# Sixteen of 22 row tiles of a down projection as seven products of quarters, in three of four SwiGLU half-steps

## The chip, the cores and the metric

The kernel runs on one core of a Trainium2 chip. The metric is the time of one execution on the device in microseconds (us). An engine's name is short here: PE is the tensor engine, PEld its weight load, DVE the vector engine, ACT the scalar engine, POOL the GpSimd engine, SP the engine whose queue issues the transfers.

## The reference: what is computed

A two-layer encoder trunk on 512 tokens of width 1024. Each layer has a SwiGLU half-step, a token mixer and another SwiGLU half-step, each followed by a layer norm. The change concerns the second, third and fourth of the four half-steps (the first one keeps its code). Cut to that, the reference is

```
def swiglu(x, w_gate, w_up, w_down):            # [512,1024], [1024,2816] twice, [2816,1024]
    return (jax.nn.silu(x @ w_gate) * (x @ w_up)) @ w_down

x = layer_norm(DEEPNORM_ALPHA * x + 0.5 * swiglu(x, w_gate[l, i], w_up[l, i], w_down[l, i]),
               ln_g[l, 2 * i], ln_b[l, 2 * i])
```

## The kernel before, in words

Tokens lie in NT = 4 tiles of 128 and the hidden width 2816 in NF = 22 row tiles of 128. Every float32 product is three products of float32r numbers: each operand is split into hi (a rounded copy, made by ACT in `split`, line 90) and lo = x - hi (made by DVE, line 92), and `mm3` (lines 122 to 124) sums hi*hi, hi*lo and lo*hi in PSUM. A product of one 128x128 stationary tile with 512 columns is thus three matmul instructions.

`ffn` is one half-step. Its up part runs over fg = 0 to 10, two row tiles of the hidden width at a time: four weight loads of 512 KB (two of the gate weights, two of the up weights), each split into a pair of tiles `whi`, `wlo`, then 96 matmuls of 512 columns into four PSUM banks. ACT's tanh (line 251) and three DVE operations (lines 252 and 254, and the lo of the split) turn the four banks into the activations `act` of two row tiles, hi and lo. At fg = 0 some token tiles of x are still to be transposed; there the columns are worked in two halves of 256 tokens, with the transposes (`flush`, line 131) between them.

Its down part runs over the 22 row tiles of `w_down`: one load of 512 KB, one split, and 4 token tiles x 2 column halves x 3 = 24 matmuls into all eight PSUM banks. The last four row tiles are held back and done token tile by token tile, so that the layer norm of one token tile (`ln_tile`) runs under the next one's matmuls. `ln_tile` begins with two DVE operations (line 158) that add 0.25 times a bank to `xt`, the tile that holds alpha*x; `self.pending` then keeps the transposes of the normed tile for the next stage.

The weights come through pools that turn round: four `raw` buffers (`fetch`, line 104), five `whi` and five `wlo` (`halves`), eight PSUM banks. A load is issued by SP when DVE has finished with the `raw` buffer it gets, and ACT splits into a `whi` when the matmuls that read it are done. Every engine takes its instructions in a fixed order that a scheduler has written down at build time; only in a block under `as_written` is PE's order the order of the program. In the half-steps 2 to 4 of the kernel before nothing is under `as_written`.

Of the kernel before, what the change touches and what calls it, by code (L numbers as in the profile page):

```python
# [2 lines left out]

# [12 lines left out]
P = 128  # L16
# [31 lines left out]
class Trunk:  # L48
    """Every float32 product runs as three float32r passes: each operand is split exactly into
    hi (rounded to float32r) and lo = x - hi, and hi*hi + hi*lo + lo*hi is summed in PSUM."""  # L50
# [21 lines left out]
    @contextmanager  # L72
    def as_written(self, *engines):
        """The engines take what the block traces in the order of the program."""
# [38 lines left out]
    def load_next(self):  # L113
        """the next phase's first weights, ahead of it"""
        if self.coming:
            self.got, got = [], self.got
            got.append(self.load(*self.coming.pop(0)))
            self.got = got

    def mm3(self, ps, ah, al, bh, bl, start, stop):  # L120
        mm = self.nc.tensor.matmul
# [14 lines left out]
    def rstd(self, var, scale, eps):  # L136
        """(scale*var + eps) ** -0.5 on [128, 1]"""
# [13 lines left out]
    def ln_tile(self, t, z, p0, p1, yscale, g, b, out=None, spill=None):  # L151
        """z holds alpha*x of token tile t; x <- LayerNorm(z + yscale*y), then alpha*x into z.
        The transposes wait in self.pending, so that the tensor engine has other work first."""
        nc = self.nc
        s = self.sm.tile([P, 6], F32, name="st")
        for h, p in enumerate((p0, p1)):
            zz = z[:, h * 512:(h + 1) * 512]
            nc.vector.scalar_tensor_tensor(out=zz, in0=p, scalar=yscale, in1=zz, op0=ALU.mult, op1=ALU.add,
                                           accum_out=s[:, h:h + 1])
# [3 lines left out]
        for h, p in enumerate((p0, p1)):  # L163
# [23 lines left out]
    def flush(self, keep=0):  # L187
        """the waiting transposes, but for the last few"""
# [3 lines left out]
    def cols(self, bks, stat, a=0, b=SEQ):  # L192
        """Products of weight columns with x^T, for tokens a..b."""
# [5 lines left out]
    def load_x(self, x, xt):  # L199
        """x and the first weights; the transposes of the later tokens wait in self.pending"""  # L200
# [79 lines left out]

    def out_proj(self, W, stat, order, get_z, g_ap, b_ap, spill=None):
        """x <- LayerNorm(alpha*x + y @ W), y given transposed as [hi, lo] tiles of 128 rows.
        Runs up to the next yield with each step; stat[c] must be there when chunk c has its turn."""
# [38 lines left out]
    def gelu2(self, y, out, tmp):  # L322
        """out = 2*gelu(y) (tanh form); y may be in PSUM, out and tmp in SBUF."""
# [880 lines left out]
```

## Time and profile before

| | |
|---|---|
| median of 3 runs | 1848.93 us (1847.23 to 1849.03) |
| span of the profiled execution, first to last instruction | 1845.7 us |
| what lies around the span, median less span | 3.2 us |
| PE busy, PEld busy | 1818.3 us, 1523.2 us |
| DVE busy, ACT busy | 898.4 us, 637.0 us |
| matmul instructions | 8896 |
| mean granted clock of PE | 0.998 of full speed |

Busy time counts an instruction from its start to its end, and instructions of one engine that follow closely overlap a little: a distance from start to start is what an engine needs per instruction in a dense stretch. A share of the span is a mean over stages with different limits, so the stage itself has to be looked at.

### The profile page before, as it was taken

The page shows a single profiled execution, that of the slowest core. Times are in us where ns is not written, and L with a number is a line of the kernel's source. Part 1 is how long each engine was busy: PE and PEld are TensorE (multiplying, and loading weights), DVE is VectorE, ACT ScalarE, POOL GpSimd, SP SyncE. Part 2 cuts the span into 40 slices and gives each one's busy share as a digit, 9 for nine tenths or more (in the row PEclk, how much of TensorE's full clock was granted, in tenths as well). Part 3 has the DMA queues.
Part 4 walks back from the last instruction along what each step waited for, and adds up shares of the span by engine and source line. Part 5 has one row for each costly group of instructions (what it writes and reads, how often), then busy time and mean ns, then how long its engine had stood idle before and what let it go on. Part 6 is the DMA issues. An engine that isn't in the chain of part 4 may idle for free.

```text
span 1845.7 us, 22332 instructions
## 1 busy us (share of the span) xinstructions
PE 1818.3 (99%) x8896; PEld 1523.2 (83%) x8896; DVE 898.4 (49%) x1531; ACT 637.0 (35%) x971; POOL 32.2 (2%) x119
## 2 busy tenths in 40 slices
PE   8999999999999999999999999999999999999998
PEld 7888888888877888888889888888878898888886
DVE  7856542267766644433227334432388554343324
ACT  3233421246675432222115223221264332222211
POOL 0000000000000000000000000000010000000000
PEclk9999999999999999999999999999999999999999
DMA  6345623264412633332323333323333153333231
GB/s 206 105 125 166 205 96 103 91 193 132 153 55 92 205 115 100 95 102 93 98 97 104 102 94 100 97 98 93 118 101 104 47 149 92 103 92 103 92 103 57
DMA packets 158968, 206.48 MB, mean 112 GB/s; under 512 B 7696, under 2 KB 129808, under 8 KB 158864
## 3 DMA queue, kind: packets, MB, share of 16 engines
q1 hardware_dynamic: 158864, 205.06, 36.3%
q8 instruction: 69, 1.13, 0.3%
q14 instruction: 35, 0.29, 0.0%
HBM read 189.83 MB, written 14.16 MB: 111 GB/s over the span
## 4 chain that ended last, share of the span: by engine, by line
PE 72%; issue 22%; DVE 3%; ACT 1%; DMA 1%; POOL 1%; POOLq 0%; SPq 0%; DVEq 0%; ACTq 0%
PE ps L122 23%; PE ps L123 23%; PE ps L124 23%; PE ps L131 1%; PE ps L650 1%; DVE wlo L92 1%; DMA s5tl<-side 1%; PE ps L698 0%; POOL rs L141 0%; PE ps L690 0%; DMA x<-in_x_dram 0%; DVE pl L92 0%; ACT ps L164 0%; PE ps L689 0%; ACT whi L90 0%
## 5 line engine op out<-in xcount | busy, mean ns | idle before, releaser
L92 DVE TENSOR_TENSOR wlo<-raw,whi 128x1024 fp32r<-128x1024 f32 x313 | 382.6, 1222 | 593.0 <-ACT whi L90 592.0
L122 PE MATMUL ps<-xh,whi 128*128 128x512 f32 (+1 forms) x1696 | 635.9, 376 | 0.7 <-ACT xh L90 0.7
L123 PE MATMUL ps<-xl,whi 128*128 128x512 f32 (+1 forms) x1696 | 633.4, 374 | 2.8 <-DVE xl L92 2.8
L124 PE MATMUL ps<-xh,wlo 128*128 128x512 f32 (+1 forms) x1696 | 633.2, 374 | 0.0
L90 ACT ACTIVATE whi<-raw 128x1024 fp32r<-128x1024 f32 x313 | 330.7, 1058 | 823.0 <-PE ps L123 470.3
L122 PEld LDWEIGHTS ps<-xh,whi 128*128 128x128 f32 x1696 | 319.2, 189 | 59.8 <-issue 3.1
L123 PEld LDWEIGHTS ps<-xl,whi 128*128 128x128 f32 x1696 | 320.3, 189 | 58.0 <-DVE xl L92 3.3
L124 PEld LDWEIGHTS ps<-xh,wlo 128*128 128x128 f32 x1696 | 320.2, 189 | 56.7
L122 PE MATMUL ps<-whi,act 128*128 128x512 f32 x656 | 255.5, 390 | 0.0
L124 PE MATMUL ps<-whi,act 128*128 128x512 f32 x656 | 255.2, 389 | 0.0
L123 PE MATMUL ps<-wlo,act 128*128 128x512 f32 x656 | 255.2, 389 | 0.0
L124 PEld LDWEIGHTS ps<-whi,act 128*128 128x128 f32 x656 | 123.2, 188 | 25.5
L123 PEld LDWEIGHTS ps<-wlo,act 128*128 128x128 f32 x656 | 123.2, 188 | 25.4
L122 PEld LDWEIGHTS ps<-whi,act 128*128 128x128 f32 x656 | 123.2, 188 | 25.4
L252 DVE SCALAR_TENSOR_TENSOR th<-th,ps 128x512 f32<-128x512 f32 x88 | 59.8, 683 | 113.4 <-ACT th L251 113.4
L251 ACT ACTIVATE th<-ps 128x512 f32<-128x512 f32 x88 | 51.9, 595 | 155.1 <-PE ps L124 155.1
L254 DVE TENSOR_TENSOR th<-th,ps 128x512 f32<-128x512 f32 x88 | 59.7, 686 | 92.8 <-PE ps L124 92.8
L92 DVE TENSOR_TENSOR act<-th,act 128x512 fp32r<-128x512 f32 x82 | 52.7, 684 | 0.0
L122 PE MATMUL ps<-whi,xh 128*128 128x256 f32 (+1 forms) x160 | 49.6, 312 | 2.0 <-ACT whi L90 1.5
L123 PE MATMUL ps<-wlo,xh 128*128 128x256 f32 (+1 forms) x160 | 49.1, 307 | 2.2 <-DVE wlo L92 2.2
L90 ACT ACTIVATE act<-th 128x512 fp32r<-128x512 f32 x82 | 47.2, 617 | 7.6 <-DVE th L254 7.5
L124 PE MATMUL ps<-whi,xl 128*128 128x256 f32 (+1 forms) x160 | 48.5, 304 | 0.0
(303 smaller groups left out, 1360.2 us busy)
## 6 DMA issues: line engine op xcount, KB each, us to landing
raw<-in_wg_dram SPq DMA_DIRECT2D x88, 512.0 KB, 3.8
raw<-in_wu_dram SPq DMA_DIRECT2D x88, 512.0 KB, 3.8
raw<-in_wd_dram SPq DMA_DIRECT2D x88, 512.0 KB, 3.2
raw<-in_ab_in_dram SPq DMA_DIRECT2D x20, 512.0 KB, 4.5
raw<-in_cd_in_dram SPq DMA_DIRECT2D x12, 512.0 KB, 3.7
x<-in_x_dram SPq DMA_DIRECT2D x8, 512.0 KB, 6.7
s<-zf SPq DMA_DIRECT2D x8, 512.0 KB, 5.2
raw<-in_ab_out_dram SPq DMA_DIRECT2D x8, 512.0 KB, 4.2
```

The lines of the kernel that those rows point to most:

```text
L90: nc.scalar.activation(out=hi, in_=src, func=AF.Copy, scale=scale)
L92: nc.vector.tensor_tensor(out=lo, in0=src, in1=hi.bitcast(F32), op=ALU.subtract)
L122: mm(ps, ah, bh, start=start, stop=False)
L123: mm(ps, ah, bl, start=False, stop=False)
L124: mm(ps, al, bh, start=False, stop=stop)
L131: self.nc.tensor.transpose(p[:, j * P:(j + 1) * P], src[:, k * P:(k + 1) * P], self.ident)
L251: nc.scalar.activation(out=th, in_=bk[0, f], func=AF.Tanh, scale=0.5)
L252: nc.vector.scalar_tensor_tensor(out=th, in0=th, scalar=1.0, in1=bk[0, f], op0=ALU.add, op1=ALU.mult)
L254: nc.vector.tensor_tensor(out=th, in0=th, in1=bk[1, f], op=ALU.mult)
L650: nc.tensor.matmul(banks[h][:, o:o + w], a[r, i * P:i * P + P], b[r, :w], start=n == 0, stop=n == 2)
```

## The change

The half-steps 2 to 4 call `ffn7` instead of `ffn`. The first sixteen row tiles of the down part, in two groups of four pairs (pair j holds row tiles 2j and 2j+1), are no longer multiplied tile by tile. For a group, the activations are a 2x2 matrix of blocks (256 tokens by the even or the odd row tiles) and the weights a 2x2 matrix of blocks (even or odd row tiles by 512 columns), and the product of the two is made from seven products of blocks in place of eight (Winograd's form of Strassen's method). The factors are blocks or sums of blocks. The sums of activations are made by DVE at the end of each `up(fg)` (lines 345 to 348, into `hb`), so that a slot `sl` holds seven stationary factors, hi and lo, for a pair. The sums of weights are made by DVE from four loads (`w21`, `w11`, `w12`, `w22`, lines 384 to 387). A group has two units of two pairs. The seven products go, in the order of the code, into four pairs of banks Y, Z, X, V, and `take` adds a pair of banks to `xt` (line 162, the same operation as line 158 before); X is read out three times and V twice, and further products are summed onto what the banks hold. A group runs as soon as its fourth `up` is done: after fg = 3 and after fg = 7. Row tiles 16 to 21 are done as before. The whole of the up part and the two groups stand under `as_written`, so PE follows the program's order there. The lines that are only docstrings and comments, and were taken out, change nothing.

```diff
+    def add_to(self, zz, p, scale, total=None):
+        self.nc.vector.scalar_tensor_tensor(out=zz, in0=p, scalar=scale, in1=zz, op0=ALU.mult, op1=ALU.add,
+                                            **({} if total is None else {"accum_out": total}))
...
+    def ffn7(self, xt, wg, wu, wd, g_ap, b_ap, out=None, fetch=None, groups=(4, 4), res=4):
+        wv = wd.rearrange("(j two p) d -> two p j d", two=2, p=P)
+        b11, b12, b21, b22 = (wv[i][:, :, c:c + 512] for i in range(2) for c in (0, 512))
...
+            def slot():
+                return ap.tile([P, 2, 7, 256], F32R, tag="sl", name="sl", bufs=max(groups))
+            def up(fg):
...
+                    else:
+                        tt(out=hb[:, 0::7] if f == 0 else hb[:, 1:3], in0=th.rearrange("p (a c) -> p a c", a=2),
+                           in1=bk[1, f].rearrange("p (a c) -> p a c", a=2), op=ALU.mult)
...
+                tt(out=hb[:, 3], in0=hb[:, 7], in1=hb[:, 2], op=ALU.subtract)
+                tt(out=hb[:, 5], in0=hb[:, 0], in1=hb[:, 7], op=ALU.subtract)
+                tt(out=hb[:, 4], in0=hb[:, 3], in1=hb[:, 0], op=ALU.subtract)
+                tt(out=hb[:, 6], in0=hb[:, 1], in1=hb[:, 4], op=ALU.add)
+                slots[fg] = sl = slot()
+                self.split(hb[:, 0:7], sl[:, 0], sl[:, 1])
+            def part(b, banks, js, w, start, stop, onto=False):
+                hi, lo = w
+                for i, j in enumerate(js):
+                    for t in range(2):
+                        c = slice(t * P, t * P + P)
+                        self.mm3(banks[t], slots[j][:, 0, b, c], slots[j][:, 1, b, c], hi[:, i], lo[:, i],
+                                 start and i == 0, stop and i == len(js) - 1, onto)
+            def down(gi):
...
+                for u in units:
+                    shape, rows = [len(u), 512], slice(u[0], u[-1] + 1)
+                    at_end = u is units[0], u is units[-1]
+                    w11, w12 = (ap.tile([P] + shape, F32, tag=n, name=n, bufs=2) for n in ("b11", "b12"))
+                    w21 = self.fetch(b21[:, rows], shape)
+                    p2 = self.halves(w21, shape)
+                    nc.sync.dma_start(w11, b11[:, rows])
+                    p1 = self.halves(w11, shape)
+                    nc.sync.dma_start(w12, b12[:, rows])
+                    w22 = self.fetch(b22[:, rows], shape)
+                    t1 = self.w.tile([P] + shape, F32, tag="raw", name="raw", bufs=RAW)
+                    tt(out=t1, in0=w11, in1=w12, op=ALU.add)
+                    tt(out=w12, in0=w12, in1=w22, op=ALU.add)
+                    tt(out=w11, in0=w11, in1=w12, op=ALU.add)
+                    tt(out=w21, in0=w21, in1=w11, op=ALU.add)
+                    q4 = self.halves(w21, shape)
+                    q5 = self.halves(t1, shape)
+                    part(1, Y, u, p2, *at_end)
+                    part(2, Z, u, q4, *at_end)
+                    part(0, X, u, p1, *at_end)
+                    part(3, V, u, q5, *at_end)
+                    held.append((u, shape, rows, w11, w12))
+                take(Y, 0, 0, 0.25)
+                take(Z, 1, 0, 0.25)
+                take(X, 0, 0, 0.25)
+                take(V, 1, 1, 0.25)
+                for u, shape, rows, w11, w12 in held:
+                    part(4, X, u, self.halves(w11, shape), False, u is units[-1], True)
+                take(X, 0, 1, -0.25)
+                for u, shape, rows, w11, w12 in held:
+                    part(6, V, u, self.load(b22[:, rows], shape), False, u is units[-1], True)
+                take(V, 0, 1, 0.25)
+                for u, shape, rows, w11, w12 in held:
+                    part(5, X, u, self.halves(w12, shape), False, u is units[-1], True)
+                take(X, 1, 1, -0.25)
+                take(X, 1, 0, 0.25)
+            with self.as_written(mybir.EngineType.PE):
+                for fg in range(NF // 2):
+                    up(fg)
+                    if fg == 0 and fetch is not None:
+                        xt = fetch()
+                    if fg + 1 in first:
+                        down(first.index(fg + 1) - 1)
...
-        k.ffn(xt, wg[0, 1], wu[0, 1], wd[0, 1], ln_g[0, 2], ln_b[0, 2], fetch=x_back)
+        k.ffn7(xt, wg[0, 1], wu[0, 1], wd[0, 1], ln_g[0, 2], ln_b[0, 2], fetch=x_back)
...
-        k.ffn(xt, wg[1, 0], wu[1, 0], wd[1, 0], ln_g[1, 0], ln_b[1, 0])
+        k.ffn7(xt, wg[1, 0], wu[1, 0], wd[1, 0], ln_g[1, 0], ln_b[1, 0])
...
-        k.ffn(xt, wg[1, 1], wu[1, 1], wd[1, 1], ln_g[1, 2], ln_b[1, 2], out=out)
+        k.ffn7(xt, wg[1, 1], wu[1, 1], wd[1, 1], ln_g[1, 2], ln_b[1, 2], out=out)
```

The built programs show three places. The first is PE at the end of `up(3)` of the second half-step. Before, the last matmuls of that step (bank ps_6247) are followed by those of `up(4)` (the gate weights whi_6324, x in xh and xl):

```order
L122 MATMUL ps_6247<-xh_69,whi_6256 128x512
L123 MATMUL ps_6247<-xl_70,whi_6256 128x512
L124 MATMUL ps_6247<-xh_69,wlo_6257 128x512
L122 MATMUL ps_6320<-xh_69,whi_6324 128x512
L123 MATMUL ps_6320<-xl_70,whi_6324 128x512
```

Now, at the same place, they are followed by the first group's products: bank ps_6318 is the first of Y, whi_6330 and wlo_6331 are the split of `w21`, and sl_5891 and sl_6035 are the slots of fg = 0 and fg = 1.

```order
L124 MATMUL ps_6241<-xh_69,whi_6250 128x512
L125 MATMUL ps_6241<-xl_70,whi_6250 128x512
L126 MATMUL ps_6241<-xh_69,wlo_6251 128x512
L124 MATMUL ps_6318<-whi_6330,sl_5891 128x512
L125 MATMUL ps_6318<-wlo_6331,sl_5891 128x512
L126 MATMUL ps_6318<-whi_6330,sl_5891 128x512
L124 MATMUL ps_6319<-whi_6330,sl_5891 128x512
L125 MATMUL ps_6319<-wlo_6331,sl_5891 128x512
L126 MATMUL ps_6319<-whi_6330,sl_5891 128x512
L124 MATMUL ps_6318<-whi_6330,sl_6035 128x512
```

A group of 168 such matmuls now stands between `up(3)` and `up(4)`, and another between `up(7)` and `up(8)`.

The second place is DVE at the same point of the second half-step. Before, from the last step of `up(3)` on, it has the two multiplications that empty the banks, two weight splits of `up(4)` and the two splits of the activations:

```order
L254 TENSOR_TENSOR th_6308<-th_6308,ps_6246 128x512
L254 TENSOR_TENSOR th_6314<-th_6314,ps_6247 128x512
L92 TENSOR_TENSOR wlo_6461<-raw_6458,whi_6460 128x1024
L92 TENSOR_TENSOR act6_5644<-th_6308,act6_5644 128x512
L92 TENSOR_TENSOR act7_5645<-th_6314,act7_5645 128x512
L92 TENSOR_TENSOR wlo_6467<-raw_6464,whi_6466 128x1024
```

Now the first of those two multiplications is followed by this (wlo_6408, wlo_6413, wlo_6425 and wlo_6429 are the four weight splits of the second unit, wlo_6489 and wlo_6505 those for `part(4)` of both units, ps_6318 and ps_6319 are Y, sl_6315 is the slot of fg = 3):

```order
L341 TENSOR_TENSOR hb_6302<-th_6307,ps_6241 128x512
L346 TENSOR_TENSOR hb_6302<-hb_6302 128x256
L345 TENSOR_TENSOR hb_6302<-hb_6302 128x256
L93 TENSOR_TENSOR wlo_6408<-raw_6405,whi_6407 128x1024
L347 TENSOR_TENSOR hb_6302<-hb_6302 128x256
L348 TENSOR_TENSOR hb_6302<-hb_6302 128x256
L93 TENSOR_TENSOR wlo_6413<-b11_6403,whi_6412 128x1024
L386 TENSOR_TENSOR b11_6403<-b11_6403,b12_6404 128x1024
L93 TENSOR_TENSOR sl_6315<-hb_6302,sl_6315 128x1792
L387 TENSOR_TENSOR raw_6405<-raw_6405,b11_6403 128x1024
L93 TENSOR_TENSOR wlo_6425<-raw_6405,whi_6424 128x1024
L93 TENSOR_TENSOR wlo_6429<-raw_6419,whi_6428 128x1024
```

Behind it, between the read-outs of Y, Z and X, stand the splits for the later products (`take` of X, ps_6322 and ps_6323, comes behind the split wlo_6525 of the second load of b22):

```order
L93 TENSOR_TENSOR wlo_6489<-b11_6326,whi_6488 128x1024
L162 SCALAR_TENSOR_TENSOR xb0_5628<-ps_6318,xb0_5628 128x512
L162 SCALAR_TENSOR_TENSOR xb1_5629<-ps_6319,xb1_5629 128x512
L93 TENSOR_TENSOR wlo_6505<-b11_6403,whi_6504 128x1024
L162 SCALAR_TENSOR_TENSOR xb2_5630<-ps_6320,xb2_5630 128x512
L162 SCALAR_TENSOR_TENSOR xb3_5631<-ps_6321,xb3_5631 128x512
L93 TENSOR_TENSOR wlo_6525<-raw_6522,whi_6524 128x1024
L162 SCALAR_TENSOR_TENSOR xb0_5628<-ps_6322,xb0_5628 128x512
L162 SCALAR_TENSOR_TENSOR xb1_5629<-ps_6323,xb1_5629 128x512
```

The whole program has 8880 matmul instructions before and 8736 now, and SP issues 473 transfers before and 485 now.

The third place is PE at the start of the second half-step (it reads the same in the third and the fourth), behind the transposes of the last token tile. Before, the scheduler put six products with xh ahead of the first that needs xl:

```order
L131 MATMUL ps<-ident,zf 128x128 x8
L122 MATMUL ps<-xh,whi 128x256 x4
L122 MATMUL ps<-xh,whi 128x512 x2
L123 MATMUL ps<-xl,whi 128x256
L124 MATMUL ps<-xh,wlo 128x256
```

Now the order is that of the program, and the second product behind the transposes needs xl:

```order
L133 MATMUL ps<-ident,zf 128x128 x8
L124 MATMUL ps<-xh,whi 128x256
L125 MATMUL ps<-xl,whi 128x256
L126 MATMUL ps<-xh,wlo 128x256
L124 MATMUL ps<-xh,whi 128x256
```

## Rows read from the trace of the kernel before

**Rows 1.** The page: span, and busy time and instructions of each engine.

```profile
span 1845.7 us, 22332 instructions
...
PE 1818.3 (99%) x8896; PEld 1523.2 (83%) x8896; DVE 898.4 (49%) x1531; ACT 637.0 (35%) x971; POOL 32.2 (2%) x119
```

**Rows 2.** Chain that ended last, by line: within 1010 to 1342 us (third half-step).

```profile
by line: PE ps L123 33.3%; PE ps L124 33.3%; PE ps L122 33.1%; PE ps L131 0.3%
```

**Rows 3.** Busy time by stretch: first half-step, third's up, third's down (columns first).

```profile
core 0: us, PE busy (x) PEld busy (x) DVE busy (x) ACT busy (x) POOL busy (x), PEclk, DMA share, GB/s
30.00:80.00 50.00, 50.00 (x257) 42.93 (x256) 46.06 (x180) 17.09 (x21) 0.00 (x0) 1.00 0.38 113
1010.00:1228.00 218.00, 218.00 (x968) 180.73 (x967) 88.31 (x102) 62.60 (x80) 0.00 (x0) 1.00 0.35 102
1240.00:1327.00 87.00, 87.00 (x385) 72.06 (x384) 19.61 (x16) 16.98 (x17) 0.00 (x0) 1.00 0.31 97
```

**Rows 4.** Timeline of DVE in the third half-step: two steps of its up part.

```profile
1086.89 0.69 DVE L252 SCALAR_TENSOR_TENSOR th<-th,ps 128x512 f32<-128x512 f32 x1 [3.30 <-ACT th L251]
...
1108.65 0.69 DVE L252 SCALAR_TENSOR_TENSOR th<-th,ps 128x512 f32<-128x512 f32 x1 [3.30 <-ACT th L251]
```

**Rows 5.** Timeline of DVE, third half-step: first and last of 17 down-weight splits.

```profile
1240.40 1.23 DVE L92 TENSOR_TENSOR wlo<-raw,whi 128x1024 fp32r<-128x1024 f32 x1 [4.26 <-ACT whi L90]
...
1327.39 1.23 DVE L92 TENSOR_TENSOR wlo<-raw,whi 128x1024 fp32r<-128x1024 f32 x1 [4.21 <-ACT whi L90]
```

**Rows 6.** Groups by line and shape: count, busy us, mean ns, idle before.

```profile
L92 DVE TENSOR_TENSOR wlo<-raw,whi 128x1024 fp32r<-128x1024 f32 x312 | 381.9, 1224 | 593.0 <-ACT whi L90 592.0
L254 DVE TENSOR_TENSOR th<-th,ps 128x512 f32<-128x512 f32 x88 | 59.7, 686 | 92.8 <-PE ps L124 92.8
L92 DVE TENSOR_TENSOR act<-th,act 128x512 fp32r<-128x512 f32 x82 | 52.7, 684 | 0.0
L158 DVE SCALAR_TENSOR_TENSOR xb<-ps,xb 128x512 f32<-128x512 f32 x32 | 22.1, 690 | 23.6 <-PE ps L124 23.5
L90 ACT ACTIVATE whi<-raw 128x1024 fp32r<-128x1024 f32 x312 | 330.1, 1059 | 822.5 <-PE ps L123 470.3 <-PE ps L124 332.5 <-issue 12.2
L251 ACT ACTIVATE th<-ps 128x512 f32<-128x512 f32 x88 | 51.9, 595 | 155.1 <-PE ps L124 155.1
L90 ACT ACTIVATE act<-th 128x512 fp32r<-128x512 f32 x82 | 47.2, 617 | 7.6 <-DVE th L254 7.5
```

**Rows 7.** Timeline of DVE in a dense stretch of the second mixer.

```profile
1390.08 0.68 DVE L92 TENSOR_TENSOR ml<-pm,mh 128x512 fp32r<-128x512 f32 x1
1390.68 0.68 DVE L1056 TENSOR_TENSOR pad<-pad 128x512 f32<-128x512 f32 x1
1391.28 1.21 DVE L92 TENSOR_TENSOR wlo<-raw,whi 128x1024 fp32r<-128x1024 f32 x1
1392.42 0.68 DVE L1056 TENSOR_TENSOR pad<-pad 128x512 f32<-128x512 f32 x1
```

**Rows 8.** The page: DMA issues, KB each, us from issue to landing.

```profile
raw<-in_wg_dram SPq DMA_DIRECT2D x88, 512.0 KB, 3.8
...
raw<-in_wd_dram SPq DMA_DIRECT2D x88, 512.0 KB, 3.2
```

**Rows 9.** Timeline of all engines, start of the second half-step.

```profile
633.27 1.04 PE L131 MATMUL ps<-ident,zf 128*128 128x128 f32 x8
633.91 1.09 ACT L90 ACTIVATE xh<-ps 128x512 fp32r<-128x512 f32 x2 [3.64 <-PE ps L131]
634.54 1.29 DVE L92 TENSOR_TENSOR xl<-ps,xh 128x512 fp32r<-128x512 f32 x2 [3.02 <-ACT xh L90]
634.56 1.21 PE L122 MATMUL ps<-xh,whi 128*128 128x256 f32 x6 [0.25 <-ACT xh L90]
...
635.60 0.28 PE L123 MATMUL ps<-xl,whi 128*128 128x256 f32 x1
```

**Rows 10.** Who waited for whom, whole span: us, times, longest us.

```profile
DVE wlo L92 <- ACT whi L90: 592.0, 248, 5.1
ACT whi L90 <- PE ps L123: 470.3, 132, 7.8
ACT whi L90 <- PE ps L124: 333.1, 83, 4.6
```

More of the change, by code (lines that the diff above doesn't have):

```diff
@@ L2 @@
 from contextlib import contextmanager
+from functools import partial
 import concourse.bass as bass
@@ L118, in load_next, with mm3 @@
             self.got = got
-    def mm3(self, ps, ah, al, bh, bl, start, stop):
-        mm = self.nc.tensor.matmul
+    def mm3(self, ps, ah, al, bh, bl, start, stop, onto=False):
+        mm = partial(self.nc.tensor.matmul, skip_group_check=onto)
         mm(ps, ah, bh, start=start, stop=False)
@@ L151, in ln_tile, with ln_rest @@
     def ln_tile(self, t, z, p0, p1, yscale, g, b, out=None, spill=None):
-        nc = self.nc
         s = self.sm.tile([P, 6], F32, name="st")
         for h, p in enumerate((p0, p1)):
-            zz = z[:, h * 512:(h + 1) * 512]
-            nc.vector.scalar_tensor_tensor(out=zz, in0=p, scalar=yscale, in1=zz, op0=ALU.mult, op1=ALU.add,
-                                           accum_out=s[:, h:h + 1])
+            self.add_to(z[:, h * 512:(h + 1) * 512], p, yscale, s[:, h:h + 1])
+        self.ln_rest(t, z, s, (p0, p1), g, b, out, spill)
+    def add_to(self, zz, p, scale, total=None):
+        self.nc.vector.scalar_tensor_tensor(out=zz, in0=p, scalar=scale, in1=zz, op0=ALU.mult, op1=ALU.add,
+                                            **({} if total is None else {"accum_out": total}))
+    def ln_rest(self, t, z, s, junk, g, b, out=None, spill=None):
+        nc = self.nc
         nmu = s[:, 2:3]
@@ L162, in ln_tile @@
                                        op0=ALU.add, op1=ALU.mult)
-        for h, p in enumerate((p0, p1)):
+        for h, p in enumerate(junk):
             nc.scalar.activation(out=p, in_=z[:, h * 512:(h + 1) * 512], func=AF.Square, bias=nmu,
```

68 lines of the change are left out of this document (added).

## The prediction

> **What bounds the kernel now.** I read the page's busy times first: PE is busy 1818.3 of 1845.7 us [rows 1]. Since busy time of overlapping matmuls proves little, I then asked the chain of waits for one whole half-step, the third. The reader is to see that there it is nothing but the three matmul lines [rows 2]: no load, no split and no read-out of a bank ever ends a wait. The third view, busy time by stretch, shows the same for both parts of that half-step, with DVE at 88.31 of 218 us in the up part and 19.61 of 87 us in the down part, and PE at its upper clock level (granted 1.00, which is 2.4 GHz) [rows 3]. The list of waits shows from the other side that the helpers wait for PE: ACT waited 470.3 and 333.1 us for matmuls to free a `whi`, and DVE 592.0 us for ACT [rows 10]. So a half-step lasts as long as its matmuls, and the change is worth what it takes from PE, less what the new work makes PE wait.
>
> **What one matmul is worth.** In the up part the same DVE instruction returns after 1108.65 - 1086.89 = 21.76 us [rows 4], in which PE does 96 matmuls: 226.7 ns each. In the down part 17 splits, one per row tile, span 1327.39 - 1240.40 = 86.99 us [rows 5], 5.437 us for 24 matmuls: 226.5 ns. I take 226.5.
>
> A page speaks against that price: the Trainium skill, "TensorE: Matmul & The Clock Gate", section "Back-to-back issue gap", states about 131 ns per 512-column matmul in a sustained stream with weight loads. By it the 144 matmuls below would be worth 18.9 us, by the rows 32.6. The trace does not agree with it (226.5 ns), and the sum goes by the trace.
>
> **What is removed.** Sixteen row tiles cost 16 x 24 = 384 matmuls before. A group now takes 7 products x 4 pairs x 2 token tiles x 3 = 168, two groups 336. That is 48 fewer per half-step and 144 in all, as the built programs say (8880 and 8736). 144 x 0.2265 = **32.6 us**, if PE never waits. Stationary tiles, columns and weight loads of a matmul have the same shapes as in the down part before, so its price stays.
>
> **What is added for DVE.** Per group, from the last step of `up(2)` to the last read-out (one up of 21.76 us and a group of 168 x 0.2265 = 38.1 us, 59.8 us together), DVE has 24 operations on 1024 columns (weight splits, the four of `up(4)` among them, and weight sums), 20 on 512 that read a bank for `take` or `hb`, 2 for tanh, 8 sums on 256 and 2 splits on 1792. The first two kinds have rows: 1224 ns, and 683 to 690 ns [rows 6]. The other two lie on the line through 512 and 1024 columns, (1224 - 684)/512 = 1.055 ns per column: 0.41 us for 256 and 2.03 us for 1792 (estimates; the bounds are the 684 ns row above and the 1224 ns row below, since more columns don't take less time). 24 x 1.224 + 20 x 0.69 + 2 x 0.68 + 8 x 0.41 + 2 x 2.03 = 51.9 us of 59.8: 87%. Closely following rows overlap: a 512-column one returns after 0.60 us, a 1024-column one after 1.14 [rows 7], which makes it about 48 us, 80%. DVE has to be walked through, then, but is not over full.
>
> **The walk through a group.** Time 0 is the end of `up(3)` on PE. A `part` is 12 matmuls, 2.72 us; the first unit's Y, Z, X, V end at 2.72, 5.44, 8.15, 10.87, the second's at 13.6, 16.3, 19.0, 21.7; then come the later products onto X (to 27.2), V (32.6) and X (38.1).
> - *Before 0.* The first unit needs its four splits. `up(2)`'s multiplications begin at -21.5. Adding up the rows in DVE's order, with ACT's copy (1.06 us [rows 6]) ahead of each split and a `whi` free only when PE is done with it, the sums and the splits of `w21`, `w11`, the sum `w21` and `t1` are through at about -3.0. DVE then waits for PE's end with 3 us in hand.
> - *Slot of fg = 3.* Two multiplications, four sums, two splits and one weight sum stand before its lo. ACT's copy of 1792 columns is 617 + 1280 x 0.863 = 1.72 us (estimate, same line through ACT's rows [rows 6]). With full durations the lo is there at 9.0, and Y's second unit needs it at 10.87 + 1.4 = 12.2.
> - *Z's second unit* needs the split of its sum at 13.6; it comes at 12.5 (full durations) or 11.7 (overlapped). What is queued behind it on DVE are the next splits and the read-outs, and PE waits for those.
> - *The first read-out of X* is the tightest: X's second unit ends at 19.0, and the products onto X start at 21.7. DVE has the splits for `part(4)`, the read-outs of Y and Z and one split of b22 ahead of it; it ends at 20.3 (overlapped) or 21.5 (full). Later read-outs have over 3 us.
> - *After the group* `up(4)` takes the banks of Y and Z, read out by 18, and finds its first weights split.
>
> So PE waits 0 us by the overlapped rows. The upper bound: 0.1 us of hand-over on each of the 22 DVE rows between 0 and the read-out of X brings it to 23.7 for the second bank, needed at 22.4: with the semaphore's own time up to 1.7 us. I take 0.25 us, near the lower end because dense DVE rows do overlap; six groups: **+1.5 us**, bounds 0 and 10.2.
>
> **The starts of the half-steps.** Behind the transposes of the last token tile PE used to run six products on xh in 1.04 us (634.56 to 635.60) before it needed xl [rows 9]. Now the second product needs it. xl's first half takes 0.69 of its 1.29 us for two, until 635.23, and one xh product lasts 0.12, until 634.68: PE waits 0.55 us, three times: **+1.7 us** (bounds 0 and 3 x 1.0).
>
> **Costed at nothing.** SP issues 12 more loads (b22 is loaded twice), and `b11` and `b12` of the first unit stand ahead of the last `x_back` load in its queue; a load lands in 3.2 to 3.8 us [rows 8] and the `raw` buffers are asked for most of an up ahead. If that cover goes, one landing is the price (second rival). ACT gets 14 copies of 1024 and one of 1792 per group, 16.5 us of 38. An `up` has 4 x 0.41 + 2.03 - 2 x 0.68 = 2.3 us more of DVE, hidden under its 21.76 us of matmuls, of which DVE used 40% [rows 3]. Layer norms, the mixers and the six row tiles at the end are as before.
>
> **Sum.** 1845.7 - 32.6 + 1.5 + 1.7 = 1816.3 us of span, and with the 3.2 us around it **1819.5 us** (median before 1848.93, -29.4 us, 1.6%).
>
> **Rivals.**
> - *Hand-overs slip in every group.* The upper bound above, 10.2 in place of 1.5 us: 1848.9 - 32.6 + 1.7 + 10.2 = 1828.2. For it: ACT and DVE take turns on each weight, and the margins are 1 to 1.5 us. Against: DVE overlaps closely where it is dense [rows 7].
> - *Loads come late.* If a unit's last load misses its turn by one landing in each group, 6 x 3.2 = 19.2 us: 1848.9 - 32.6 + 1.7 + 19.2 = 1837.2. Against: ACT waits for PE, not for loads [rows 10].
> - *A matmul left out is worth only the page's price*, because weight loads and matmuls of neighbours hide one another: 1848.9 - 18.9 + 1.7 + 1.5 = 1833.2. The row tiles' even 5.437 us speak against it: nothing in that stretch is hidden.
> - *DVE becomes the bound, and the kernel slower.* The place is the up before each group and the group itself. If each of the 24 weight rows waits for ACT's copy instead of finding it done, DVE's 51.9 us grow; from (59.8 + 5.2 - 51.9)/24 = 0.55 us of wait per row on (5.2 us is the sixth part of 30.9, that is 32.6 less 1.7), the gain is gone. At 0.75 us: (51.9 + 18 - 59.8) x 6 = 60.6 us against 30.9: 1878.6. For it: 248 of DVE's splits do wait for ACT now [rows 10]. Against: they do since ACT waits for PE, and in the first half-step DVE is busy 46.06 of 50 us while PE doesn't lose anything [rows 3].
>
> **Chances and range.** A matmul's price and their number are certain within 1%, so the forecast (1816 to 1824) has 0.78, the hand-overs 0.11, late loads 0.04, the page's price 0.01; DVE as the bound 0.06, of which 0.02 fall near no change. What a measurement of this kernel tells from no change is about 0.2%, 3.7 us. Faster 0.94, same 0.02, slower 0.04. The range, 1815 to 1830, takes in no wait at all at the starts and in the groups (1848.9 - 32.6 = 1816.3, less a us for the spread of the runs) and the first rival.
>
> **What would show it.** Matmuls 144 fewer, and 226.5 ns from start to start inside the groups; a group of 38 to 39 us between `up(3)` and `up(4)`; PE's waits for line 162 or line 93 in a group under 2 us; about 0.5 us of PE waiting for xl at the three starts; DVE near 80% busy in a group's stretch, and about 1120 us in all (898.4 plus some 75 per half-step). The prediction is wrong if PE's row spacing grows in the groups, if the first read-out of X or a split stops PE for several us, or if loads end waits of ACT or DVE there.

## The result, and the profile after

The changed kernel takes 1817.15 us (median of 4 runs, 1816.2 to 1818.47), the kernel before in the same session 1848.31 us (4 runs, 1847.23 to 1849.03): a ratio of 0.9835, with a 95% interval of 0.9821 to 0.9849, 31.2 us less. The forecast was 29.4 us less.

The page of the profiled execution, to be held against [rows 1]: span, busy time and number of instructions of each engine.

```profile
span 1815.5 us, 22309 instructions
...
PE 1786.5 (98%) x8752; PEld 1497.6 (82%) x8752; DVE 1104.4 (61%) x1783; ACT 690.4 (38%) x983; POOL 32.1 (2%) x119
```

PE has 144 instructions less and 31.8 us less of busy time, and the span is 30.2 us shorter. DVE has 206 us more work (1104.4 against 898.4), which shows nowhere in the span.

Where the 30.2 us come from can be read off the transposes that open each half-step. The timeline of PE has the last eight of them at these times (three of the rows, for the second, third and fourth half-step):

```profile
634.19 1.03 PE L133 MATMUL ps<-ident,zf 128*128 128x128 f32 x8
...
988.28 1.03 PE L133 MATMUL ps<-ident,zf 128*128 128x128 f32 x8
...
1467.13 1.03 PE L133 MATMUL ps<-ident,zf 128*128 128x128 f32 x8
```

The kernel before has them at 633.27 [rows 9] and at these two times:

```profile
997.64 1.04 PE L131 MATMUL ps<-ident,zf 128*128 128x128 f32 x8
...
1487.06 1.04 PE L131 MATMUL ps<-ident,zf 128*128 128x128 f32 x8
```

From one to the next, the second half-step went from 364.37 to 354.09 us (-10.28), the third with the second mixer from 489.42 to 478.85 (-10.57), and the fourth, to the end of the span, from 358.64 to 348.37 (-10.27). Together -31.1 us, nearly the same amount three times. The first half-step, which isn't changed, was 0.9 us longer in this execution; that is scatter (in the runs below these transposes stand between 632.85 and 635.06 us). The three intervals scatter far less: in the control below they are 354.09, 478.85 and 348.41 us, so they tell more than the medians do.

Busy time by stretch shows what the groups are like (the first group of the second half-step, and the up step ahead of it):

```profile
core 0: us, PE busy (x) PEld busy (x) DVE busy (x) ACT busy (x) POOL busy (x), PEclk, DMA share, GB/s
713.00:751.00 38.00, 38.00 (x169) 31.51 (x168) 30.62 (x36) 16.23 (x15) 0.00 (x0) 1.00 0.50 152
690.00:712.00 22.00, 22.00 (x99) 18.23 (x98) 15.64 (x17) 7.03 (x7) 0.00 (x0) 1.00 0.16 52
```

DVE is busy 30.62 of 38 us (81%) in the group, and PE all 38 us, at granted clock 1.00. The group's first product starts at 713.00 us and the first one of `up(4)` at 751.08: 38.08 us for 168 matmuls, 226.7 ns each. The groups by line and shape confirm it. The columns are count, busy us, mean ns of one, idle time before:

```profile
L124 PE MATMUL ps<-whi,sl 128*128 128x512 f32 x480 | 187.2, 390 | 0.0
L126 PE MATMUL ps<-whi,sl 128*128 128x512 f32 x480 | 186.9, 389 | 0.0
L125 PE MATMUL ps<-wlo,sl 128*128 128x512 f32 x480 | 186.9, 389 | 0.0
L162 DVE SCALAR_TENSOR_TENSOR xb<-ps,xb 128x512 f32<-128x512 f32 x128 | 83.0, 683 | 23.5 <-PE ps L126 23.4
L93 DVE TENSOR_TENSOR sl<-hb,sl 128x1792 fp32r<-128x1792 f32 x24 | 48.6, 2023 | 31.9 <-ACT sl L91 31.9
L91 ACT ACTIVATE sl<-hb 128x1792 fp32r<-128x1792 f32 x24 | 40.8, 1700 | 44.6 <-DVE hb L348 44.6
```

The 0.0 at the end of the first three rows is the answer to the main question: PE never waited ahead of any of the 1440 matmuls on slots (the groups' 1008, and 432 of the six row tiles that are left). The reader can see from the other rows that it is the helpers who wait. The two longest entries of PE's list of waits for the whole span are these (us, times, longest us):

```profile
PE ps L133 <- DMA x<-in_x_dram: 6.0, 2, 4.5
PE ps L125 <- DVE xl L93: 4.0, 5, 2.1
```

Before, the second one read

```profile
PE ps L123 <- DVE xl L92: 2.8, 2, 2.1
```

so three new waits came, 1.2 us together. They are the three starts. The timeline there shows the second product behind the transposes start 0.73 us behind the first (in [rows 9] six ran in a row there):

```profile
635.47 0.39 PE L124 MATMUL ps<-xh,whi 128*128 128x256 f32 x1 [0.25 <-ACT xh L91]
636.20 0.39 PE L125 MATMUL ps<-xl,whi 128*128 128x256 f32 x1 [0.34 <-DVE xl L93]
```

### The profile page after: what moved, and what is told of

It reads as the page before. It is cut to its first block, busy times and chain, and to the rows that moved or that the text cites. A ratio compares the mean times of both kernels' runs of the same rounds, so it can differ in the third digit from the quotient of the medians.

```text
span 1815.5 us, 22309 instructions
## 1 busy us (share of the span) xinstructions
PE 1786.5 (98%) x8752; PEld 1497.6 (82%) x8752; DVE 1104.4 (61%) x1783; ACT 690.4 (38%) x983; POOL 32.1 (2%) x119
## 4 chain that ended last, share of the span: by engine, by line
issue 60%; PE 33%; DVE 3%; ACT 1%; DMA 1%; POOL 1%; POOLq 0%; SPq 0%; DVEq 0%; ACTq 0%
PE ps L124 10%; PE ps L125 10%; PE ps L126 10%; PE ps L810 1%; DVE wlo L93 1%; POOL rs L143 1%; DMA s5tl<-side 1%; PE ps L858 0%; PE ps L850 0%; PE ps L133 0%; DMA x<-in_x_dram 0%; DVE pl L93 0%; PE ps L849 0%; ACT ps L173 0%; POOL st L177 0%
## 5 line engine op out<-in xcount | busy, mean ns | idle before, releaser
L124 PEld LDWEIGHTS ps<-xh,whi 128*128 128x128 f32 x1696 | 320.6, 189 | 59.8 <-issue 3.1
L124 PE MATMUL ps<-whi,sl 128*128 128x512 f32 x480 | 187.2, 390 | 0.0
L126 PE MATMUL ps<-whi,sl 128*128 128x512 f32 x480 | 186.9, 389 | 0.0
L125 PE MATMUL ps<-wlo,sl 128*128 128x512 f32 x480 | 186.9, 389 | 0.0
L126 PEld LDWEIGHTS ps<-whi,sl 128*128 128x128 f32 x480 | 90.2, 188 | 18.7
L125 PEld LDWEIGHTS ps<-wlo,sl 128*128 128x128 f32 x480 | 90.2, 188 | 18.5
L124 PEld LDWEIGHTS ps<-whi,sl 128*128 128x128 f32 x480 | 90.2, 188 | 18.4
L162 DVE SCALAR_TENSOR_TENSOR xb<-ps,xb 128x512 f32<-128x512 f32 x128 | 83.0, 683 | 23.5 <-PE ps L126 23.4
L93 DVE TENSOR_TENSOR sl<-hb,sl 128x1792 fp32r<-128x1792 f32 x24 | 48.6, 2023 | 31.9 <-ACT sl L91 31.9
L341 DVE TENSOR_TENSOR hb<-th,ps 128x512 f32<-128x512 f32 x48 | 32.6, 687 | 56.0 <-PE ps L126 56.0
L91 ACT ACTIVATE sl<-hb 128x1792 fp32r<-128x1792 f32 x24 | 40.8, 1700 | 44.6 <-DVE hb L348 44.6
L91 ACT ACTIVATE whi<-b 128x1024 fp32r<-128x1024 f32 x36 | 38.1, 1059 | 39.6 <-PE ps L126 38.2
L93 DVE TENSOR_TENSOR wlo<-b,whi 128x1024 fp32r<-128x1024 f32 x36 | 44.0, 1221 | 14.2 <-ACT whi L91 14.2
```

The source lines that it names most:

```text
L91: nc.scalar.activation(out=hi, in_=src, func=AF.Copy, scale=scale)
L93: nc.vector.tensor_tensor(out=lo, in0=src, in1=hi.bitcast(F32), op=ALU.subtract)
L124: mm(ps, ah, bh, start=start, stop=False)
L125: mm(ps, ah, bl, start=False, stop=False)
L126: mm(ps, al, bh, start=False, stop=stop)
L162: self.nc.vector.scalar_tensor_tensor(out=zz, in0=p, scalar=scale, in1=zz, op0=ALU.mult, op1=ALU.add, **({} if total is None else {"accum_ ...
```

## The experiments

Eleven kernels ran, in three sets (e0 to e3, e4 to e7, e8 to e10), each set beside the kernel before on the same chip (1847.71, 1847.78 and 1847.76 us). The theory is that of the prediction: a matmul left out is worth 226.5 ns, since PE doesn't wait in a group; the starts cost about half a us each; DVE, ACT and the loads have room. The main rivals are that a matmul is worth less, that a part of the gain comes from PE's new order, and that the groups stand close to an edge which the time doesn't show.

### e0_after_again: the changed kernel once more, as the control

> The changed kernel itself, as the control of this set. Theory: 144 matmuls at 226.5 ns (32.6 us) less some 1.2 us of waits for xl at three starts and nothing in the groups, so about 31 us below the kernel before, ratio 0.983.

Measured: 1815.93 us (1813.43 to 1817.99, 5 runs), ratio 0.9825 [0.9812, 0.9838], 31.8 us less. The differences below are taken from it.

### e1_free_start: the first up step outside the fixed order

```diff
+            up(0)
+            if fetch is not None:
+                xt = fetch()
             with self.as_written(mybir.EngineType.PE):
-                for fg in range(NF // 2):
+                for fg in range(1, NF // 2):
                     up(fg)
-                    if fg == 0 and fetch is not None:
-                        xt = fetch()
```

> The changed kernel with the first up step of each half-step taken out of as_written, so that the scheduler may again put products with xh ahead of the first that needs xl. Theory (the waits for xl at the starts are lost time): 1.2 to 1.7 us faster than the control, and PE's waits for xl at the three starts gone from the list of waits. Rival (such a wait is made good later, or the groups lose as much): within 0.3 us of the control.

Measured: 1815.4 us (1814.15 to 1815.76, 4 runs), ratio 0.9822 [0.9809, 0.9836]. The timeline of PE has five products on xh in a row again, and the list of waits has the old 2.8 us:

```profile
634.13 0.97 PE L124 MATMUL ps<-xh,whi 128*128 128x256 f32 x5 [0.25 <-ACT xh L91]
```

```profile
PE ps L125 <- DVE xl L93: 2.8, 2, 2.1
```

The waits at the starts are thus an effect of the fixed order. In the medians they are not told from nothing: 0.5 us lies inside the scatter of the runs. The intervals from transposes to transposes do tell:

```profile
632.85 1.04 PE L133 MATMUL ps<-ident,zf 128*128 128x128 f32 x8
...
986.34 1.04 PE L133 MATMUL ps<-ident,zf 128*128 128x128 f32 x8
...
1464.60 1.04 PE L133 MATMUL ps<-ident,zf 128*128 128x128 f32 x8
```

With the span of 1812.4 us they are 353.49, 478.26 and 347.80 us, each 0.6 us shorter than the control's, 1.8 us together. A start costs more than the 0.4 us that the list counts for it, since a product that runs alone takes longer as well (0.39 us, where they start 0.12 us apart in a row).

### e2_order_alone: the kernel before, with the new order and nothing else

```diff
-            with self.as_written(*([mybir.EngineType.PE] if late else [])):
+            with self.as_written(mybir.EngineType.PE):
```

> The kernel before with PE in the program's order in the up part of the half-steps 2 to 4, and nothing else. Theory: 1.2 to 1.7 us slower than the kernel before, the price of the three starts. Rival (program order is free): no difference, and then the 1.4 us between 32.6 and the measured gain lie in the groups.

Measured: 1849.09 us (1846.65 to 1849.94, 11 runs), ratio 1.0005 [0.9996, 1.0014]: between 0.7 us faster and 2.6 us slower than before. The waits for xl are 4.0 us in 5, as in the changed kernel. No part of the gain comes from the order. Whether it costs the predicted 1.7 us or nothing the medians don't tell. The intervals do: the last transposes start at 633.88, 998.85 and 1488.80 us and the span is 1848.0, so the three are 364.97, 489.95 and 359.20 us, 0.60, 0.53 and 0.56 above those of the kernel before, 1.7 us in all.

### e3_one_step: the seven products in the third half-step alone

```diff
-        k.ffn7(xt, wg[0, 1], wu[0, 1], wd[0, 1], ln_g[0, 2], ln_b[0, 2], fetch=x_back)
+        k.ffn(xt, wg[0, 1], wu[0, 1], wd[0, 1], ln_g[0, 2], ln_b[0, 2], fetch=x_back)
...
-        k.ffn7(xt, wg[1, 1], wu[1, 1], wd[1, 1], ln_g[1, 2], ln_b[1, 2], out=out)
+        k.ffn(xt, wg[1, 1], wu[1, 1], wd[1, 1], ln_g[1, 2], ln_b[1, 2], out=out)
```

> Only the third half-step as seven products, the second and the fourth as before. Theory (every half-step gives 48 matmuls, less one start): a third of the whole, 10.9 - 0.4 = 10.5 us below the kernel before. Rival (one of the other half-steps gains more or less, for instance the second for its loads of x): the third gives under 9 or over 12 us.

Measured: 1837.15 us (1834.66 to 1838.4), ratio 0.994 [0.9927, 0.9952], 10.6 us less than before: a third of the control's 31.8. The half-steps add up and don't disturb one another: the third interval is 478.81 us, as in the control, and the other two are 364.37 and 358.67, as in the kernel before.

### e4_eighth_back: one product of each unit done twice

```diff
                     part(1, Y, u, p2, *at_end)
+                    part(1, Y, u, p2, False, False, True)
```

> The changed kernel with the product of the second row block done twice in each unit (onto Y again, so the output is not the reference's): 24 matmuls more per group, 144 in all, which is what the change took away, and no other work. Theory (a matmul costs its 226.5 ns in a group as elsewhere): 32.6 us slower than the control, within 2 us of the kernel before. Rival (a matmul more is worth only the page's 131 ns, or hides under DVE's work in a group): 19 us or less.

Measured: 1849.5 us (1848.55 to 1851.51), ratio 1.001 [1.0, 1.0019], 33.6 us above the control for 144 matmuls: 233 ns each, with the scatter of both medians (about 1.5 us) 223 to 244. That takes in the 226.5 ns of the rows and is far from the rival's 131. The intervals are sharper: with the last transposes at 633.59, 998.56 and 1488.23 us and a span of 1847.5 they are 364.97, 489.67 and 359.27 us, together 32.6 us above the control's, 226 ns for each matmul.

### e5_rows8 and e6_rows16: more rows for DVE

In each unit 8 or 16 additions of 512 columns go into a tile that nobody reads. In the program they stand ahead of the split of Z's factor; in DVE's order the scheduler spreads them. In the second unit of the first group with 8 rows, two stand ahead of that split and the others between it and the read-out of X, and the splits for `part(4)`, which stood ahead of the read-outs of Y and Z, come behind that of X.

```diff
+            junk = ap.tile([P, 512], F32, name="junk")
...
+                    for _ in range(8):
+                        tt(out=junk, in0=w21[:, 0], in1=w11[:, 0], op=ALU.add)
                     q4 = self.halves(w21, shape)
```

> The changed kernel with eight additions of 512 columns more on DVE per unit, into a tile that nobody reads: 16 per group, 9.6 to 11 us of DVE each group. Theory (DVE has 4 us of idle time before the group and 1.2 us in it, and the margins of the walk take the rest): PE waits 0.3 to 0.7 us per group, 2 to 4 us slower than the control. Rival (the groups are already bound by DVE): the whole of the added DVE time, 58 us or more.

Measured, 8 rows: 1816.95 us (1816.69 to 1818.12), ratio 0.9836 [0.9822, 0.9851], 1.0 us above the control. The first group, by stretch:

```profile
713.00:751.00 38.00, 38.00 (x169) 31.47 (x168) 35.75 (x45) 16.35 (x15) 0.00 (x0) 1.00 0.52 168
```

DVE is busy 35.75 of 38 us (94%; 9 of the 16 added rows fall in this stretch), and PE still all of them; no wait of PE lies between 1000 and 1320 us. The intervals are 354.11, 478.80 and 348.43 us, within 0.1 us of the control's. So the theory, which allowed 2 to 4 us, gave the added rows too much.

> The same with sixteen additions per unit: 19 us of DVE per group, which makes its work 67 us in a stretch of 59.8, and the scheduler now puts a split that PE needs behind the first read-out of Y. Theory: DVE becomes the bound, at least 7.4 us of PE waiting per group and some 3 us more for the order, 44 to 62 us slower than the control, so slower than the kernel before. Rival (PE would not wait for DVE there): under 10 us.

Measured, 16 rows: 1869.66 us (1867.13 to 1870.69), ratio 1.0122 [1.0105, 1.0139], 53.7 us above the control. PE's waits:

```profile
PE ps L125 <- DVE wlo L93: 25.6, 14, 3.4
PE ps L124 <- ACT whi L91: 12.1, 7, 1.8
```

There is the edge, and the fourth rival's mechanism: PE stands behind DVE's splits, and behind ACT's copies, some of which read DVE's sums. The waits are only a part of the price: PE is also busy 1802.4 us in place of 1786.5 with the same matmuls, and between 733 and 753 us, behind two such waits and around a third, the granted clock is 0.91. The edge lies between 8 and 16 rows of 0.6 us per unit, 10 to 19 us of DVE per group and the up ahead of it. The changed kernel has at least 9.6 us in hand, if the scheduler may place the rows; rows at one fixed place were not tried.

### e7_442: a third group, of one unit

Row tiles 16 to 19 join in as a group of two pairs right behind `up(9)`, and only two row tiles are left for the layer norm's stage. That takes 36 further matmuls away.

```diff
-    def ffn7(self, xt, wg, wu, wd, g_ap, b_ap, out=None, fetch=None, groups=(4, 4), res=4):
+    def ffn7(self, xt, wg, wu, wd, g_ap, b_ap, out=None, fetch=None, groups=(4, 4, 2), res=2):
```

(with e1's edit, as in e9 and e10)

> A version that might beat both: four more row tiles as seven products (groups of 4, 4 and 2 pairs), two row tiles at the end instead of six, with the free start. 36 matmuls fewer, 8.2 us, but the last row tiles now give PE 2.7 us per token tile under which a layer norm of 4.2 us of DVE and the next stage's splits have to lie. Theory: the tail gives the gain back, 2 to 6 us per half-step: 2 us faster to 10 us slower than the control. Rival (the norms are hidden under the next stage's first products): 8 us faster.

Measured: 1848.61 us (1846.19 to 1852.08, 10 runs), ratio 1.0004 [0.9995, 1.0014], 32.7 us above the control, far outside what was expected. What PE waits for:

```profile
PE ps L124 <- ACT sl L91: 14.9, 6, 3.8
PE ps L126 <- DVE sl L93: 3.2, 3, 1.3
PE ps L133 <- DVE zf L185: 5.7, 4, 1.5
```

Three of the six waits in the first row (3.75 us each) and the second row are one mechanism. In a group of two units the slot of the last `up` is first read by the second unit, 12 us later. With a single unit it is read after six matmuls, and PE stops for DVE's sums, ACT's copy of 1792 columns and DVE's lo. The timeline of PE has the place, and the price of such a stop:

```profile
919.84 0.39 PE L126 MATMUL ps<-whi,sl 128*128 128x512 f32 x1
923.98 0.75 PE L124 MATMUL ps<-whi,sl 128*128 128x512 f32 x1 [3.75 <-ACT sl L91]
924.52 0.63 PE L125 MATMUL ps<-wlo,sl 128*128 128x512 f32 x1
926.04 0.79 PE L126 MATMUL ps<-whi,sl 128*128 128x512 f32 x1 [0.89 <-DVE sl L93]
926.63 0.63 PE L124 MATMUL ps<-whi,sl 128*128 128x512 f32 x1
927.06 0.63 PE L125 MATMUL ps<-wlo,sl 128*128 128x512 f32 x1
...
930.90 0.40 PE L125 MATMUL ps<-wlo,sl 128*128 128x512 f32 x1
```

Behind the wait a matmul takes 0.63 us in place of 0.39, and the next starts 0.43 us later in place of 0.23. The columns by stretch, two of them, last but two the granted clock:

```profile
926.00:928.00 2.00, 1.96 (x5) 1.58 (x6) 0.69 (x1) 0.00 (x0) 0.00 (x0) 0.50 0.00 0
930.00:932.00 2.00, 2.00 (x8) 1.57 (x7) 0.95 (x2) 0.00 (x0) 0.00 (x0) 0.78 0.16 24
```

From 919.84 to the matmul at 930.90 there are 14 starts, which take 14 x 0.2265 = 3.2 us elsewhere and 11.1 here. Of the 7.9 us lost, 4.6 are the two waits, and 3.3 the slower matmuls at granted clock 0.50, which is 1.2 GHz. The other three waits of the first row (1.44, 1.44 and 0.76 us) stand behind `up(10)`: both row tiles of its slot are the ones held back, so that it too is read at once.

### e9_442_late: the third group behind the last up step

The edit to e7's kernel:

```diff
-                    if fg + 1 in first:
+                    if fg + 1 in first[:-1]:
                         down(first.index(fg + 1) - 1)
+                down(2)
```

> The groups of 4, 4 and 2 pairs again, with the third group after the last up step, so that the slot of its second pair is ready when PE comes to it. Theory (what cost the version before was PE's wait for that slot, 3.75 us, and the matmuls at the lower clock level behind it): both are gone, 8.2 us of matmuls saved less 1 to 3 us per half-step of tail: 1811 to 1818 us, between 5 us faster and 2 us slower than the control. Rival (the tail of two row tiles is the larger part of what was lost): over 1830 us.

Measured: 1821.59 us (1819.13 to 1822.58), ratio 0.9856 [0.9842, 0.9871]: 27.0 us less than e7, and all waits for `sl` are gone, which shows the slots as the cause: three stops of 7.9 us and the 3.6 us behind `up(10)` are 27.3. But it is 5.7 us above the control, and misses the 1811 to 1818 that were expected. What was left is in the layer norms' stage, with `zf` the normed tile that the next half-step's transposes read:

```profile
PE ps L133 <- DVE zf L185: 7.4, 4, 2.4
```

### e10_res2: two row tiles left, no third group

e1's kernel with `res=2`: of the six row tiles that are multiplied as usual, two are held back for the layer norms in place of four.

> The changed kernel with the free start and with only two row tiles held back for the end of a half-step instead of four, the same matmuls otherwise. This is the tail alone. Theory: 1 to 3 us per half-step, 3 to 9 us slower than the control, with PE waiting for the norm. Rival (the tail's price is large, since PE's waits there bring its clock down): over 12 us.

Measured: 1830.95 us (1828.55 to 1832.74), ratio 0.9908 [0.9894, 0.9923], 15.6 us above e1, with not one matmul more or less. That is far above the theory's 3 to 9 us, and in the rival's range. The end of the second half-step, by stretch, here and then in e1:

```profile
960.00:980.00 20.00, 15.72 (x75) 12.41 (x75) 14.73 (x28) 11.37 (x21) 2.48 (x9) 0.95 0.45 157
980.00:985.00 5.00, 5.00 (x25) 5.00 (x25) 4.64 (x6) 2.56 (x6) 1.04 (x2) 0.51 0.04 10
```

```profile
960.00:980.00 20.00, 20.00 (x122) 17.77 (x121) 16.26 (x26) 12.82 (x22) 2.78 (x9) 1.00 0.15 40
980.00:985.00 5.00, 5.00 (x44) 5.00 (x43) 4.32 (x5) 3.04 (x5) 0.00 (x0) 1.00 0.93 290
```

Two row tiles are too few to cover four layer norms. PE is idle 4.3 us in these stretches, and while it works again the granted clock is 0.51: 25 matmuls in 5 us against 44. The clock takes 0.49 x 5 + 0.05 x 15.7 = 3.2 us, with the idle time 7.5. From the last transposes of the second half-step to those of the third it is 361.00 us against 353.49 in e1, 7.5 us more, so that is all of it there. The other two intervals are 2.9 and 5.9 us longer (481.12 against 478.26, 353.69 against 347.80). In the last half-step PE isn't held up at all: its last matmul starts 339.12 us behind the transposes in both kernels, and what grows is the time from there to the end of the span, 14.6 us in place of 8.7, in which norms stand that no matmul covers any more. So the rival's cause, the clock, is only a part of the price.

With that, the two kernels before can be added up. A third group is worth 36 x 0.2265 = 8.2 us, and its row tiles are taken from this cover: 15.6 - 8.2 is 7.4 us above e1, and e9 measured 6.2. With the 27.3 us for e7's waits on slots it is 34.7 us above e1, and e7 measured 33.2.

### e8_raw3: three load buffers in place of four

```diff
-RAW = 4
+RAW = 3
```

> The changed kernel with three raw buffers in place of four, everywhere. Every load is asked for one buffer later: in an up step some 5.4 us later, with a landing of 3.3 to 5.4 us and an up step of lead before. Theory (loads are asked for well ahead, that cover is wide): no more than 2 us slower than the control in the half-steps. Rival (loads are near their limit in the groups, the late loads of the prediction): 3.2 us per group, 19 us, or more.

Measured: 1825.59 us (1824.35 to 1827.89), ratio 0.9882 [0.9866, 0.9899], 9.7 us above the control, between the two expectations. The groups bear the theory out: between 640 and 960, 1000 and 1330, and 1480 and 1824 us PE waits for nothing. The loss lies at the borders of the stages: the intervals are 2.9, 4.9 and 0.0 us longer than the changed kernel's, and each ends behind the first products of the next half-step. Two stretches, here and then in the changed kernel: the start of the third half-step and the second mixer.

```profile
980.00:1000.00 20.00, 17.04 (x137) 16.15 (x136) 8.72 (x10) 7.89 (x12) 0.93 (x3) 1.00 0.66 220
...
1340.00:1360.00 20.00, 17.52 (x72) 13.99 (x73) 14.38 (x24) 11.39 (x18) 1.82 (x4) 0.91 0.38 109
```

```profile
980.00:1000.00 20.00, 19.41 (x162) 18.97 (x161) 10.33 (x12) 9.89 (x14) 0.93 (x3) 1.00 0.74 240
...
1340.00:1360.00 20.00, 18.67 (x85) 15.16 (x86) 19.31 (x32) 12.78 (x19) 1.91 (x4) 1.00 0.34 98
```

PE's busy time is 2.4 and 1.2 us lower in the two, and 2.1 us in a third, the start of the fourth half-step (1460 to 1480 us); in the mixer the granted clock fell to 0.91. At the start of the third half-step PE stands behind the split of a weight, which it doesn't in the changed kernel:

```profile
984.67 0.38 PE L124 MATMUL ps<-xh,whi 128*128 128x256 f32 x1 [1.62 <-ACT whi L91]
```

The page has the sum of it, span and PE's row:

```profile
span 1823.7 us, 22301 instructions
...
PE 1789.5 (98%) x8752; PEld 1498.1 (82%) x8752; DVE 1105.8 (61%) x1783; ACT 690.3 (38%) x983; POOL 33.5 (2%) x119
```

The span is 8.2 us longer than the changed kernel's. PE is idle 34.2 us in place of 29.0, which is 5.2 of them, and busy 3.0 us longer with the same matmuls, which is the rest. So the fourth buffer serves the starts of stages, where the first weights of the next one have to lie ready, and not the groups. That is shown for the start of the third half-step; in the mixer PE's longest wait is 1.92 us for an `xh`, and how that comes from the buffers wasn't followed.

## Why the prediction was right, step by step

- **What bounds the kernel.** Right. The matmuls did, and still do: PE is busy in every us of a group.
- **A matmul is worth 226.5 ns, 32.6 us in all.** Right, and shown from both sides: steps of 10.3 to 10.6 us where 48 matmuls went, 10.8 to 11.2 with the starts freed (e1; 48 x 0.2265 is 10.9), and 32.6 us in the intervals where 144 came back (e4). The page of the Trainium skill that the prediction weighed ("TensorE: Matmul & The Clock Gate", section "Back-to-back issue gap", about 131 ns) would have made it 18.9 us by estimate; no run here agrees with it.
- **The starts, 3 x 0.55 us.** Right in place, cause and size: three new waits, gone in e1, there in e2, and 1.8 and 1.7 us of the intervals with them, for 1.7 forecast. That the size fits is in part luck. The prediction took 0.12 us for the lone product and 0.55 for the wait, 0.67 from its start to that of the next; measured are 0.39 and 0.34, and 0.73 in all. In the medians the starts are within the scatter.
- **The waits in the groups, 1.5 us.** Too much: they are 0.0. That explains the forecast's distance: 32.6 - 1.8 = 30.8 us, against 31.1 in the intervals, 31.2 and 31.8 in the medians, and 29.4 forecast. In the span the forecast, 1816.3 us, is 0.8 above the 1815.5 of this execution; the 3.2 us around the span, which took a span and a median of different executions, are 1.75 here (1817.25 us for that span).
- **The walk through a group.** The timeline of DVE in the first group of the second half-step, whose time 0 is 713.0, can be laid beside it:

```profile
712.52 1.37 DVE L341 TENSOR_TENSOR hb<-th,ps 128x512 f32<-128x512 f32 x2 [2.61 <-PE ps L126]
...
719.48 2.02 DVE L93 TENSOR_TENSOR sl<-hb,sl 128x1792 fp32r<-128x1792 f32 x1
...
723.84 2.36 DVE L93 TENSOR_TENSOR wlo<-raw,whi 128x1024 fp32r<-128x1024 f32 x2 [1.21 <-ACT whi L91]
...
731.91 1.28 DVE L162 SCALAR_TENSOR_TENSOR xb<-ps,xb 128x512 f32<-128x512 f32 x2
```

  DVE was idle 2.61 us ahead of the first row (3 forecast). The slot's lo was done at 8.5 (9.0). The split for Z's second unit is the first of the two in the third row, done at 12.0 (11.7 to 12.5). The first read-out of X ended at 20.2 (20.3 by the overlapped rows), 1.5 us ahead of the products onto X. So the lower of its two ends held for the slot and for X, and Z's split lay between the two. DVE did wait for ACT on the way (1.21 us ahead of the third row), but the hand-overs that the first rival feared (0.1 us on each row, for which it had no row) didn't add up to a wait of PE. The sizes that had no row fit too: 2.023 us for the lo of 1792 columns (2.03 estimated), 1.700 for ACT's copy (1.72).
- **DVE's work** was right: 15.64 and 30.62 us in the up step and the group, 46.3 of 60 us, where the overlapped sum gave about 48 of 59.8; 1104 us in all is 1.4% under the 1120 forecast.
- **Late loads** and **DVE as the bound** didn't come. e8 took a buffer away without a wait in any group. e6 shows that DVE does become the bound, and the kernel slower than before, but only with 16 rows more per unit. The margin is wider than this rival drew it from full durations (51.9 of 59.8 us), by which 9.6 us of added rows cost 1.7 us a group; by the prediction's own overlapped sum (48) they cost nothing, and e5's intervals show nothing.

My own experiments were forecast less well than the change. e7 failed on a point that the walk through a group had named for two units (when the fresh slot is first read) and that I did not work out again for one. e9 and e10 failed because I priced the layer norms' cover at 1 to 3 us per half-step; without it e10's half-steps lost 2.9 to 7.5. e8 was missed by both expectations, since neither had looked at the borders of the stages. What is left open is whether a third group of two pairs beside four held-back row tiles would gain its 8.2 us; the hidden width has no room for it (20 + 4 of 22 row tiles), and it wasn't tried.

## What to carry to other kernels

When one engine is busy in every microsecond of a stage, work taken from it is worth its start-to-start distance in that stage, to within a few per cent, and a helper may be filled far (here to 94% of a group, in an order that the scheduler chose) as long as each hand-over is met in the walk through the order. Walk the order anew for every size of a group: a group of one unit reads at once what a group of two reads 12 us later. And before taking matmuls out of a stage that covers other work, price the cover; here it was worth 15.6 us, and the matmuls 8.2.

## What the runs showed of the hardware

A wait of PE can cost much more than its length. In e7, 4.6 us of waiting cost 7.9, since the matmuls behind it ran at a granted clock of 0.50 and 0.43 us apart in place of 0.23; in e10, 4.3 us of idle time between 960 and 980 us, in gaps of at most 1.9 us, were followed by 5 us at 0.51. Idle time alone doesn't tell: in e9 PE is idle 4.6 us in the same 20 us, in gaps of at most 2.4, and the granted clock stays at 1.00; what makes the difference no run here shows. Waits of 0.3 us at the starts of the half-steps left the clock at 1.00. And rows of DVE that follow closely cost less than their durations: the 96 additions of e5, 0.69 us each, raised its busy time by 55.3 us (1159.7 against 1104.4), 0.58 us each, and PE waited for none of it.
